# Longer pauses between the steps that make a recurrence chunk's operands

## The chip, the core and the metric

The kernel runs on one core of a Trainium2 chip. The metric is the device time of one execution in microseconds (us). The engines are TensorE (PE: matrix products and transposes), VectorE (DVE), ScalarE (ACT), GpSimd (POOL) and SyncE (SP, which here issues DMAs); each runs its own list of instructions in order, and they wait for each other through semaphores.

## The reference, cut to what matters

One layer of an encoder on 2112 tokens: 2048 of a new stream and 64 of a running one. A projection P = h @ w_in feeds a gated short convolution, an RWKV-7 recurrence and two gates; their merged output and a feed-forward network follow.

```python
h  = rms_norm(x);  proj = h @ w_in                    # 1024 -> 5376 columns
def step(s, inp):                                     # RWKV-7, per token, 8 heads of 64
    r_t, w_t, k_t, v_t, a_t, b_t = inp
    sa = einsum('bhij,bhj->bhi', s, a_t)
    s  = s * w_t + sa[..., None] * b_t + v_t[..., None] * k_t
    return s, einsum('bhij,bhj->bhi', s, r_t)
m = sigmoid(gate_A) * (conv(proj) @ w_conv_out) + sigmoid(gate_B) * (rwkv(proj) @ w_rwkv_out)
x = x + rms_norm(m @ w_o)
x = x + rms_norm((silu(up_1) * up_2) @ w_down)        # up = rms_norm(x) @ w_up
```

## The kernel before

The work has two stages. The first (`phase_a`, to about 1482 us) computes the projections and the whole recurrence. The second merges the branches and does the feed-forward part; the change does not touch it.

**The projections** are the fillers of the first stage. Their inputs are split into a high and a low half, so each product is three matmuls `mm` with 264 columns (`mm3`). A unit of one output column block and one half of a token quarter is 24 such matmuls, and the generator `projections` gives the turn back after every 12. Per column block, a weight tile is loaded by SP (`w_raw`), cast by ACT (`w_hi`) and subtracted by DVE (`w_lo`); evictions go to ACT and DVE. Between units DVE also adds pairs of feed-forward weights (`sw`, line 606, `weight_sums`).

**The recurrence** works on chunks of 64 tokens, two chunks to a group, 16 groups and a last one of a single chunk. Each group goes through three generators:
- `scan_prep` makes a chunk's operands. DVE scales the rows into `ar` and `bk` (line 700 to 705; bk's tile is named `v`). A pause follows. PE multiplies them, `pa<-ar,v` and `tr<-ar,v` (136), and DVE masks the result into `aa` and `aq` (716). A second pause follows. PE transposes `bk` (`tr<-cpack,v`), which needs the buffer `tr` that the masks have read, and computes `pu<-uv,aa`.
- `scan_solve` inverts 32x32 blocks by 31 pairs of small DVE operations (`tm`, `ti`, lines 760 and 762), sends them through DRAM (`asc`, `al`, `ttsc`, `tinv`), transposes a part (`d`, 776) and finishes with two products on PE (`pu<-d,aa`, `pu<-tinv`), each evicted by ACT (783, 790).
- `scan_chain` carries the state from chunk to chunk: `gy<-st,ar`, an add on DVE (`ysq`, 817), `pu<-ysq,tinv`, a copy on ACT (`uv`, 822), `pu<-uv,bkt`, `gy<-uv,aq`, a copy on ACT (`yt`, 837); then a norm on DVE and ACT and the transposes `tr<-cpack,yt`.

`phase_a` interleaves the three streams and the fillers by a counter, `self.t`. Every matmul adds its estimated length to it (`mm`, `transpose`), and a stream that yields a number gets its next turn when the counter has risen by that much since its turn began. So a pause is so much PE work, not time. A group's `scan_prep` may start when its projections are stored and the group two before it is through its chain. The order in which the code emits instructions gives their priority; a scheduler then settles each engine's list. When the fillers are used up, the counter rises by itself.

PSUM buffers `pa`, `tr`, `pu` and `gy` are single.

Of the kernel before, what the change touches and what calls it, by code (L numbers as in the profile page):

```python
# [34 lines left out]
WBUFS, KSTEP = 3, 4  # L35

YE, YT = 4, 10

PASSES = ((0, True, True, range(16)), (1, True, True, range(2)), (2, True, True, range(4)), (3, True, True, range(16)), (1, False, False, range(2, 16)), (2, False, False, range(4, 16)))
MIX = {1: 0, 3: 1, 10: 1}  # L40
# [45 lines left out]
class Trunk:  # L86
# [583 lines left out]
    def scan_prep(self, grp, nxt):  # L670


        nc, pool = self.nc, self.sp
        nch = grp["nch"]
        n = nch * CH
        if "sg" not in grp:
            self.scan_load(grp)
            yield 9
        if "ep" not in grp:
            self.scan_decays(grp)  # L680
        en, ep, v, r = grp["sg"], grp["ep"], grp["v"], grp["r"]
        ks = grp["ks"].rearrange("p (c s) t -> p c s t", s=3)
        kk, b_, kf = ks[:, :, 0], ks[:, :, 1], ks[:, :, 2]
        vt = self.tr()
        for p in range(4):
            self.transpose(vt[0:n, p, :], v[:, p, :], self.ident)
        uvs = []
        for c in range(nch):
            uv = pool.tile([P, 4, P], F32, name="uv", bufs=4)
            nc.scalar.copy(out=uv[64:128], in_=vt[c * CH:c * CH + CH])  # L690
            uvs.append(uv)
        yield 1
        epv = ep.rearrange("p (c j) t -> p c j t", j=nch)
        asc = self.dram.tile([nch * 16, CH // 2, CH // 2], F32, name="asc", bufs=2)
        chunks = grp["chunks"] = []
        for c in range(nch):
            t0 = c * CH
            uv = uvs[c]
            ar = pool.tile([P, 4, P], F32, name="ar", bufs=4)
            nc.vector.scalar_tensor_tensor(out=ar[:, :, 0:CH], in0=kk[:, :, t0:t0 + CH], scalar=-1.0, in1=epv[:, :, c, 0:CH],  # L700
                                           op0=ALU.mult, op1=ALU.mult)
            nc.vector.tensor_tensor(out=ar[:, :, CH:P], in0=r[:, :, t0:t0 + CH], in1=epv[:, :, c, 1:CH + 1], op=ALU.mult)
            bk = pool.tile([P, 4, P], F32, name="v", bufs=1)
            nc.vector.tensor_tensor(out=bk[:, :, 0:CH], in0=b_[:, :, t0:t0 + CH], in1=en[:, :, t0:t0 + CH], op=ALU.mult)
            nc.vector.tensor_tensor(out=bk[:, :, CH:P], in0=kf[:, :, t0:t0 + CH], in1=en[:, :, t0:t0 + CH], op=ALU.mult)
            yield 4
            aa = pool.tile([P, 8, CH], F32, name="aa", bufs=4)
            aq = pool.tile([P, 8, CH], F32, name="aq", bufs=4)
            pas = (self.psum.tile([P, 4, P], F32, name="pa", bufs=1), self.tr())
            for p in range(4):  # L710
                for b in range(2):
                    rows = slice(64 * b, 64 * b + 64)
                    self.mm(pas[b][:, p, :], bk[rows, p, :], ar[rows, p, :], start=True, stop=True)
            for b in range(2):
                for t, s0 in ((aa, 0), (aq, CH)):
                    nc.vector.tensor_tensor(out=t.rearrange("p (c b) t -> p c b t", b=2)[:, :, b, :], in0=pas[b][:, :, s0:s0 + CH],
                                            in1=self.amask[:, s0:s0 + CH].unsqueeze(1).broadcast_to([P, 4, CH]), op=ALU.mult)
            yield 4
            z = self.tr()
            for p in range(4):  # L720
                self.transpose(z[:, p, :], bk[:, p, :], self.ident)
            bkt = pool.tile([P, 4, P], F32, name="bkt", bufs=4)
            nc.scalar.copy(out=bkt, in_=z)
            cc = pool.tile([P, 4], F32, name="cc", bufs=4)
            nc.gpsimd.tensor_copy(out=cc, in_=epv[:, :, c, CH])
            for b in range(2):
                s0 = (b * nch + c) * 8
                nc.sync.dma_start(out=asc[s0:s0 + 8].rearrange("s u t -> u s t"),
                                  in_=aa[32 * b:32 * b + 32, :, 32 * b:32 * b + 32])
            pu = self.pu()  # L730
            for s in range(8):
                self.mm(pu[0:64, s, :], aa[64:128, s, :], uv[64:128, s // 2, (s % 2) * 64:(s % 2) * 64 + 64], start=True, stop=True)
            nc.scalar.copy(out=uv[0:64], in_=pu[0:64].rearrange("t (p h) i -> t p (h i)", h=2))
            chunks.append(dict(uv=uv, ar=ar, aa=aa, aq=aq, bkt=bkt, cc=cc))
            yield 1
        grp["asc"] = asc
        while nxt is not None and self.ready < nxt["off"] + nxt["nch"] * CH:
            yield 1
        if nxt is not None:
            self.scan_load(nxt)  # L740
            yield 9
            self.scan_decays(nxt)
# [743 lines left out]
```

## Time and profile before

| | us |
|---|---|
| median of 3 timed runs | 3283.89 |
| lowest, highest | 3279.99, 3292.36 |
| the profiled execution | 3272.44 |
| its span | 3270.7 |

The mean granted TensorE clock of the profiled execution is 0.981 of full speed. Times in the rows are counted from the start of its span. A matmul of the trace is shown with the time until its last result, so one that takes 0.28 us is followed by the next 0.12 us after its start.

### The profile page before, as it was taken

What the parts mean: (1) busy time and instruction counts of PE and PEld (TensorE: products, weight loads), DVE (VectorE), ACT (ScalarE), POOL (GpSimd) and SP (SyncE); (2) the same over time, 40 slices, a digit from 0 to 9 for tenths busy, and PEclk for the clock granted to TensorE, in tenths of its full rate; (3) what the DMA queues carried; (4) which work ended last, traced back from release to release, by engine and by line L of the source; (5) the groups of instructions that cost most, each with busy time, mean ns of one, the idle gap of its engine ahead of it and who ended that gap; (6) DMA issues with size and microseconds to landing.
All of it is one profiled execution on the core that took longest, in us unless ns stands there. A gap on an engine that the chain in (4) does not pass through costs nothing.

```text
span 3270.7 us, 64324 instructions
## 1 busy us (share of the span) xinstructions
PE 3119.1 (95%) x23060; PEld 3043.3 (93%) x23060; DVE 2375.4 (73%) x5091; ACT 1736.6 (53%) x3418; POOL 488.2 (15%) x906
## 2 busy tenths in 40 slices
PE   6999999999999999998999999999999999999997
PEld 6989899998889999998999989999999999999997
DVE  5866787887878778746576876776867776866657
ACT  7534664664575446534433455556645466544454
POOL 2400132132124101000000011210011200111100
PEclk9999999999999999999999999999999999999999
DMA  5787578766767677647475467778777887766675
GB/s 163 221 246 230 184 222 252 218 202 206 222 212 208 205 236 233 190 125 248 125 233 160 137 227 231 248 254 260 228 224 224 264 254 236 234 190 191 191 253 169
DMA packets 526226, 699.52 MB, mean 214 GB/s; under 512 B 111137, under 2 KB 358497, under 8 KB 525905
## 3 DMA queue, kind: packets, MB, share of 16 engines
q1 hardware_dynamic: 468528, 592.67, 59.5%
q0 software_dynamic: 25456, 72.20, 6.0%
q10 hardware_dynamic: 31920, 30.54, 2.8%
q8 instruction: 181, 2.97, 0.4%
q14 instruction: 141, 1.15, 0.1%
HBM read 522.10 MB, written 173.12 MB: 213 GB/s over the span
## 4 chain that ended last, share of the span: by engine, by line
issue 38%; PE 16%; POOL 5%; DMA 3%; DVE 2%; ACT 0%; POOLq 0%; SPq 0%; DVEq 0%; ACTq 0%
PE mm L136 14%; POOL tp_s L1229 3%; PE pu L136 1%; DMA x<-x_s 1%; POOL x_s L1088 1%; PE gy L136 1%; POOL out_y L1088 1%; POOL nb_s L1173 0%; DMA nb_s<-x 0%; DMA x_s<-r 0%; DMA gt_s<-psv 0%; DMA tp_s<-f 0%; DVE ti L762 0%; DMA out_y<-r 0%; DVE w_lo L150 0%
## 5 line engine op out<-in xcount | busy, mean ns | idle before, releaser
L136 PE MATMUL mm<-h_hi,w_hi 128*128 128x264 f32 (+1 forms) x5112 | 1586.3, 311 | 55.8 <-DVE f L1248 20.9
L136 PE MATMUL mm<-h_hi,w_lo 128*128 128x264 f32 (+1 forms) x5112 | 1558.1, 305 | 8.9 <-DVE w_lo L150 5.6
L136 PE MATMUL mm<-h_lo,w_hi 128*128 128x264 f32 (+1 forms) x5112 | 1559.5, 305 | 3.4 <-DVE h_lo L217 2.8
L136 PEld LDWEIGHTS mm<-h_hi,w_hi 128*128 128x128 f32 x5112 | 973.6, 191 | 81.6 <-DVE f L1248 25.0
L136 PEld LDWEIGHTS mm<-h_hi,w_lo 128*128 128x128 f32 x5112 | 974.7, 191 | 12.6 <-DVE w_lo L150 7.8
L136 PEld LDWEIGHTS mm<-h_lo,w_hi 128*128 128x128 f32 x5112 | 975.2, 191 | 7.7 <-DVE h_lo L217 3.6
L188 ACT CAST w_hi<-w_raw 128x512 fp32r<-128x512 f32 (+1 forms) x810 | 487.8, 608 | 535.4 <-PE mm L136 322.5
L189 DVE TENSOR_TENSOR w_lo<-w_raw,w_hi 128x512 fp32r<-128x512 f32 (+1 forms) x810 | 540.4, 674 | 259.9 <-ACT w_hi L188 251.7
L136 PE MATMUL mm<-t_hi,w_hi 128*128 128x352 f32 x1116 | 360.8, 323 | 1.7 <-ACT mm L1330 1.7
L136 PE MATMUL mm<-t_lo,w_hi 128*128 128x352 f32 x1116 | 358.0, 321 | 0.0
L136 PE MATMUL mm<-t_hi,w_lo 128*128 128x352 f32 x1116 | 358.0, 321 | 0.0
L150 DVE TENSOR_TENSOR w_lo<-w_raw,w_hi 128x1024 fp32r<-128x1024 f32 x168 | 207.5, 1236 | 116.6 <-ACT w_hi L149 112.6
L149 ACT CAST w_hi<-w_raw 128x1024 fp32r<-128x1024 f32 x168 | 175.7, 1047 | 135.1 <-PE mm L136 88.0
L136 PEld LDWEIGHTS mm<-t_hi,w_hi 128*128 128x128 f32 x1116 | 209.4, 188 | 2.6 <-ACT mm L1330 2.3
L1229 POOL DMA_DIRECT2D tp_s<-f x231 | 125.5, 543 | 576.8 <-DVE f L1248 337.1
L136 PEld LDWEIGHTS mm<-t_lo,w_hi 128*128 128x128 f32 x1116 | 209.7, 188 | 0.3
L136 PEld LDWEIGHTS mm<-t_hi,w_lo 128*128 128x128 f32 x1116 | 209.5, 188 | 0.0
L189 DVE TENSOR_TENSOR t_lo<-d,t_hi 128x352 fp32r<-128x352 f32 x198 | 97.6, 522 | 72.5 <-ACT t_hi L188 71.5
L188 ACT CAST t_hi<-d 128x352 fp32r<-128x352 f32 x198 | 91.5, 486 | 89.7 <-DMA d<-tp_s 83.9
L760 DVE TENSOR_TENSOR tm<-al,ti 128x60 f32<-128x60 f32 (+27 forms) x527 | 118.9, 226 | 10.7 <-DMA al<-asc 2.7
L762 DVE TENSOR_TENSOR ti<-ti,tm 128x60 f32<-128x60 f32 (+27 forms) x527 | 117.7, 223 | 8.5
L606 DVE TENSOR_TENSOR sw<-sw 128x512 f32<-128x512 f32 (+1 forms) x136 | 95.3, 701 | 20.4 <-DMA sw<-in_w_up 16.0
(207 smaller groups left out, 3731.7 us busy)
## 6 DMA issues: line engine op xcount, KB each, us to landing
w_raw<-in_w_in SPq DMA_DIRECT2D x168, 512.0 KB, 4.4
w_raw<-us_s SPq DMA_DIRECT2D x264, 256.0 KB, 3.2
w_raw<-in_w_up SPq DMA_DIRECT2D x198, 256.0 KB, 3.1
tp_s<-f POOLq DMA_DIRECT2D x231, 176.0 KB, 3.6
d<-tp_s SPq DMA_DIRECT2D x105, 352.0 KB, 3.9
w_raw<-ds_s SPq DMA_DIRECT2D x96, 256.0 KB, 3.5
sw<-in_w_up SPq DMA_DIRECT2D x88, 256.0 KB, 4.7
us_s<-sw SPq DMA_DIRECT2D x88, 256.0 KB, 3.6
```

Source lines behind the costliest of these rows:

```text
L136: self.nc.tensor.matmul(out, lhsT, rhs, **kw)
L149: nc.scalar.copy(out=hi[:, :kt], in_=raw[:, :kt])
L150: nc.vector.tensor_tensor(out=lo[:, :kt], in0=raw[:, :kt], in1=hi[:, :kt].bitcast(F32), op=ALU.subtract)
L188: nc.scalar.copy(out=hi, in_=x)
L189: (eng or nc.vector).tensor_tensor(out=lo, in0=x, in1=hi.bitcast(F32), op=ALU.subtract)
L606: nc.vector.tensor_tensor(out=w[x], in0=w[x], in1=w[y], op=ALU.add)
L760: nc.vector.tensor_tensor(out=tv, in0=al[0:np_, u, u + 1:32].unsqueeze(1).broadcast_to([np_, k, m]), in1=ti[0:np_, 0:k, u:u + 1].broadcast ...
L762: nc.vector.tensor_tensor(out=tu, in0=tu, in1=tv, op=ALU.add)
L1088: (nc.sync if rows else nc.gpsimd).dma_start(out=dst[d, :, t0:t0 + n], in_=x)
L1229: nc.gpsimd.dma_start(out=self.tp_s[TP[op], i], in_=x)
```

## The change

The two pauses of `scan_prep` inside a chunk, between the scaling and the products and between the masks and the transposes, go from 4 to a new constant `YP` = 7. Nothing else is edited.

```diff
 YE, YT = 4, 10
+
+YP = 7
...
             nc.vector.tensor_tensor(out=bk[:, :, CH:P], in0=kf[:, :, t0:t0 + CH], in1=en[:, :, t0:t0 + CH], op=ALU.mult)
-            yield 4
+            yield YP
...
                                             in1=self.amask[:, s0:s0 + CH].unsqueeze(1).broadcast_to([P, 4, CH]), op=ALU.mult)
-            yield 4
+            yield YP
             z = self.tr()
```

Lines behind the edit move down by 2. In the built program the distances change everywhere in the first stage. PE's list in the middle of it, at the end of the solve of the twelfth group; before, fillers stand around the second product:

```order
L136 MATMUL mm<-h_hi,w_lo 128x264
L136 MATMUL pu<-tinv 32x32 x16
L136 MATMUL mm<-h_hi,w_hi 128x264
L136 MATMUL mm<-h_lo,w_hi 128x264
L136 MATMUL mm<-h_hi,w_lo 128x264
```

And now:

```order
L138 MATMUL mm<-h_hi,w_lo 128x264
L138 MATMUL pu<-tinv 32x32 x16
L142 MATMUL tr<-cpack,v 128x128 x4
L138 MATMUL mm<-h_hi,w_hi 128x264
L138 MATMUL mm<-h_lo,w_hi 128x264
L138 MATMUL pu<-uv,aa 64x64 x8
```

The next group's second chunk has moved back until its last steps meet the solve's products of the group before.

PE's list at the end of the first stage, where the 128x352 matmuls are the first of the next stage. Before, the last group's output transposes stand behind fillers:

```order
L136 MATMUL mm<-h_hi,w_hi 128x264
L136 MATMUL mm<-h_lo,w_hi 128x264
L136 MATMUL mm<-h_hi,w_lo 128x264
L140 MATMUL tr<-cpack,yt 128x64 x4
L136 MATMUL mm<-h_hi,w_hi 128x352
```

And now:

```order
L138 MATMUL mm<-h_hi,w_lo 128x264
L138 MATMUL pu<-d_20513,aa 32x32 x8
L138 MATMUL pu<-tinv 32x32 x8
L142 MATMUL tr<-cpack,yt 128x128 x4
L138 MATMUL gy<-st_107,ar 128x128 x4
L138 MATMUL pu<-ysq,tinv 64x64 x8
L138 MATMUL pu<-uv,bkt 128x128 x4
L138 MATMUL gy<-uv,aq 64x64 x8
L142 MATMUL tr<-cpack,yt 128x64 x4
L138 MATMUL mm<-h_hi,w_hi 128x352
```

The last group's solve products and chain stand behind the last filler; before, they had fillers between them.

DVE's list at the same place, from the last operation of the last group's solve (64 partitions) on. Before:

```order
L762 TENSOR_TENSOR ti<-ti,tm 64x8
L830 TENSOR_TENSOR stmp<-pu,st_108 64x256 x2
L833 TENSOR_TENSOR st_107<-stmp,cc 64x4x64 x2
L843 TENSOR_REDUCE s_19893<-yt 128x8
L844 SCALAR_TENSOR_TENSOR yt<-s_19893,yt 128x512
L850 TENSOR_REDUCE s_19938<-ysq 128x8
L853 RECIPROCAL s_19938<-s_19938 128x8
L854 TENSOR_TENSOR yt<-yt,s_19938 128x512
L776 STREAM_TRANSPOSE d_20352<-tinv 32x256
```

And now:

```order
L764 TENSOR_TENSOR ti<-ti,tm 64x8
L819 TENSOR_TENSOR ysq<-gy,uv 64x512
L832 TENSOR_TENSOR stmp<-pu,st_107 64x256 x2
L835 TENSOR_TENSOR st_108<-stmp,cc 64x4x64 x2
L778 STREAM_TRANSPOSE d_20513<-tinv 32x256
L819 TENSOR_TENSOR ysq<-gy,uv 64x512
L832 TENSOR_TENSOR stmp<-pu,st_108 64x256 x2
L835 TENSOR_TENSOR st_107<-stmp,cc 64x4x64 x2
L845 TENSOR_REDUCE s_20396<-yt 128x8
```

Both chain steps of the group before the last have moved behind the last group's solve, the second of them also behind the transpose `d`.

## Rows read from the trace of the kernel before

**Rows 1.** The page, part 1: busy us, share of the span, instructions

```profile
PE 3119.1 (95%) x23060; PEld 3043.3 (93%) x23060; DVE 2375.4 (73%) x5091; ACT 1736.6 (53%) x3418; POOL 488.2 (15%) x906
```

**Rows 2.** PE's waits, 160 to 1485 us: us in total, times, longest

```profile
PE tr L140 <- DVE aq L716: 12.7, 6, 5.4
PE pa L136 <- DVE v L705: 9.1, 9, 3.4
...
PE tr L140 <- DVE tm L760: 3.9, 3, 2.0
...
PE pu L136 <- DVE aa L716: 3.4, 5, 1.2
PE tr L140 <- DVE ti L762: 3.1, 3, 1.2
```

**Rows 3.** Timeline of PE: start, us, instruction, [idle before <-releaser]

```profile
179.45 1.09 PE L140 MATMUL tr<-cpack,v 128*128 128x128 f32 x4 [5.44 <-DVE aq L716]
...
537.50 1.09 PE L140 MATMUL tr<-cpack,v 128*128 128x128 f32 x4 [4.36 <-DVE aq L716]
```

**Rows 4.** Timeline of DVE before the first of these waits

```profile
175.27 0.69 DVE L606 TENSOR_TENSOR sw<-sw 128x512 f32<-128x512 f32 x1 [6.22 <-DMA sw<-in_w_up]
```

**Rows 5.** Stretches: us, busy PE, PEld, DVE, ACT, POOL, PEclk, DMA share, GB/s

```profile
170.00:190.00 20.00, 14.56 (x118) 13.67 (x118) 11.28 (x22) 5.45 (x8) 2.84 (x2) 0.83 0.83 263
530.00:550.00 20.00, 15.64 (x119) 14.74 (x119) 16.77 (x36) 9.81 (x18) 1.83 (x6) 0.83 0.88 266
890.00:920.00 30.00, 26.50 (x179) 23.88 (x178) 19.00 (x54) 19.09 (x48) 3.96 (x14) 0.77 0.68 186
640.00:1130.00 490.00, 459.66 (x4146) 435.12 (x4146) 406.37 (x1053) 277.50 (x558) 124.61 (x241) 0.97 0.70 211
1440.00:1460.00 20.00, 20.00 (x166) 20.00 (x166) 4.90 (x4) 6.08 (x11) 0.18 (x1) 1.00 0.39 120
```

**Rows 6.** PE's waits, 640 to 1130 us

```profile
PE pa L136 <- DVE v L705: 7.9, 6, 3.4
PE mm L136 <- ACT w_hi L149: 4.8, 3, 2.9
...
PE pu L136 <- DVE aa L716: 2.5, 3, 1.2
...
PE tr L140 <- DVE ti L762: 2.4, 2, 1.2
...
PE tr L140 <- DVE aq L716: 0.6, 2, 0.5
PE tr L140 <- DVE tm L760: 0.5, 1, 0.5
```

**Rows 7.** Timeline of PE at the stage's end, without the fillers

```profile
1462.92 0.69 PE L136 MATMUL pu<-d,aa 32*32 32x32 f32 x16
...
1468.84 1.05 PE L136 MATMUL gy<-st,ar 128*128 128x128 f32 x8
1471.29 1.14 PE L136 MATMUL pu<-ysq,tinv 64*64 64x64 f32 x16
1473.93 1.05 PE L136 MATMUL pu<-uv,bkt 128*128 128x128 f32 x8
...
1481.97 0.43 PE L140 MATMUL tr<-cpack,yt 64*128 64x64 f32 x4 [1.33 <-DVE yt L854]
```

**Rows 8.** ACT: tile tinv (ns least/median/most), and the last chain's copy

```profile
L783 ACT COPY tinv<-pu x17: 362/575/579, 258.8 to 1463.8; 32x512 f32<-32x512 f32 x16, 32x256 f32<-32x256 f32 x1
...
1476.10 0.58 ACT L837 COPY yt<-gy 64x512 f32<-64x512 f32 x1 [3.04 <-PE gy L136]
```

**Rows 9.** Timeline of DVE: the last solve's first and last operation, the transpose

```profile
1398.67 0.17 DVE L760 TENSOR_TENSOR tm<-al,ti 64x31 f32<-64x31 f32 x1
...
1421.11 0.17 DVE L762 TENSOR_TENSOR ti<-ti,tm 64x8 f32<-64x8 f32 x1
...
1430.14 0.43 DVE L776 STREAM_TRANSPOSE d<-tinv 32x256 f32<-32x256 f32 x1 [1.47 <-DMA tinv<-ttsc]
```

## The prediction

> **What bounds the kernel now.** I began with the page [rows 1]: the reader sees TensorE (PE) at 95% of the span, VectorE (DVE) at 73%. The end is set by PE, so the change is worth what it adds to or takes from PE's idle time and slow clock. The edit touches only the first stage, up to about 1482 us, so I read PE's waits from 160 us (first chunk) to 1485 us. Five of its entries belong to the steps between which the pauses lie [rows 2]: the products `pa` waiting for `bk` (named v there), the transposes `tr` of `bk` waiting for the masks (named aq, tm or ti, whichever ran last on DVE), and `pu<-uv,aa` waiting for aa. Together 12.7 + 9.1 + 3.9 + 3.4 + 3.1 = 32.2 us. That is all the change can give back in waits.
>
> Next I asked why DVE was late, since a pause cures some causes and not others.
> - The two longest waits, 5.44 and 4.36 us [rows 3], are one cause. DVE sat for 6.22 us at a weight-sum addition whose DMA had not landed [rows 4], and the masks stood behind it.
> - From 640 to 1130 us DVE is busy 406 of 490 us [rows 5], and 7.9 + 2.5 + 2.4 + 0.6 + 0.5 = 13.9 us of the waits fall there [rows 6]: a backlog.
> - The rest, 32.2 - 9.8 - 13.9 = 8.5 us, is plain shortness of the pause.
>
> Third come the clock and the end of the stage. After long waits the granted clock drops: 0.83 over 170 to 190 us and 530 to 550 us, 0.77 over 890 to 920 us [rows 5], a mix of TensorE's two levels, 1.2 and 2.4 GHz. At the stage's end PE has projection matmuls ("fillers") to run beside the last group's recurrence almost to its last instruction; it waits there only 1.33 us [rows 7].
>
> **The change part by part.** No instruction is added or removed; only places move. The pauses count from before the step's own PE work. In the built order the products now stand mostly 72 to 84 fillers behind the group's first transposes or the previous chunk's, where 30 to 48 was common, and the transposes of bk stand 48 fillers behind the products instead of 24. A filler costs 20.00 / 166 = 0.12 us [rows 5], so the second pause gains 24 x 0.12 = 2.9 us, the first at least as much.
>
> 1. Waits behind the late DMA: 2.9 us off each of two, -5.8 us. Between 0 (the additions fall elsewhere, and as badly) and -9.8.
> 2. Waits in the backlog: a consumer that comes later finds DVE done, but DVE's work stays, and the next thing PE needs of it (low weight halves, evictions) waits instead. I take half, -7.0 us; bounds 0 and -13.9.
> 3. The short waits, the longest 2.0 us [rows 2], lie inside the added slack: -8.5 us; bounds -8.5 and 0.
> 4. Clock: the three stretches lose 20 x 0.17 + 20 x 0.17 + 30 x 0.23 = 13.7 us of full-speed work. The waits ahead of them shrink, but other waits stand beside them. I take half, -6.9 us; bounds 0 and -13.7.
> 5. A new neighbourhood. The single PSUM buffer `pu` now passes from the solve's second product to `pu<-uv,aa` with two fillers and four transposes between, in four groups; elsewhere 6 or more fillers lie between. The eviction in between takes 0.58 us on ScalarE (ACT) [rows 8] against some 2 x 0.12 + 0.43 us of cover (the nearest transposes [rows 7]), and its queue can hold it longer. I charge +2.5 us; bounds 0 and 5.
> 6. The end of the stage. Each group takes some 25 to 45 fillers more, and there are only so many. In the new order all projection matmuls are gone before the last group's solve products: these, that group's whole chain step and the previous group's output transposes stand one behind the other on PE with nothing between. I count from the last filler, F, with durations of the same steps. The previous chain's gy ends 24 fillers, 2.9 us, before F; from its copy at 1476.10 to the end of the output transposes at 1481.97 + 0.43 it took 6.3 us [rows 7, 8], so the transposes end at F + 3.6 (0.2 us for the copy to start). Then gy 1.05, DVE's add with its two hand-overs 0.9, pu 1.14, ACT's copy 0.7, the two last products 1476.10 - 1473.93 = 2.2 [rows 7, 8]: F + 9.6. Then 6.3 again: F + 15.9. The PE work inside is 2 x 0.69 + 2 x 0.43 + 1.05 + 1.14 + 2.2 = 6.6 us, so PE idles 9.3 us, where it idled 1.33: +8.0 us. DVE has a new order there too: the add that the previous chain needs stands behind all of the last group's solve, and the next add behind the transpose `d`, which waits for a trip through DRAM. In the trace 1430.14 + 0.43 - 1421.28 = 9.3 us pass from the solve's last operation to the end of that transpose [rows 9]; PE has 36 fillers (4.3 us) and 1.14 + 2.2 + 1.05 us of chain steps to run meanwhile, 8.7 us. About even, so I charge 1.5 us, and 1.3 us for small products at the lower clock: +10.8 us. Bounds 6 (the DVE order costs nothing and copies overlap better) and 20.
>
> The Trainium skill bears on step 6. Row: after the waits named above, 0.83 and 0.77 were granted [rows 5]. "TensorE: Matmul & The Clock Gate", section "What's actually happening", says that the throttled clock is the default and activity releases it. By that rule the bare end of the stage runs at 1.2 GHz throughout, doubling its 6.6 us of small products; the sum would be some 5 us worse. The trace agrees for long waits, but no row shows small products that trickle like this.
>
> Everything after this stage is the same program and starts behind the last chain as before; I cost it at nothing. If its first loads come sooner relative to the chain's end, that is a gain of at most a few us, left in the range.
>
> **Sum**: -5.8 - 7.0 - 8.5 - 6.9 + 2.5 + 10.8 = -14.9 us. The profiled execution ran 3272.44 us, so it would take 3257.5; it stands 11.5 us under the median of the timed runs, 3283.89. The same step from the median: 3269.0 us, 0.45% less.
>
> **Rivals.**
> - *All waits vanish.* For it: the slack added is 2.9 us and more, and most waits are under that. Against: the two longest exceed it, and DVE is 83% busy where 13.9 us of them lie. -32.2 - 13.7 + 8.0 = -37.9 us: about 3246.
> - *The waits only move.* DVE's backlog sets the pace in the passages where PE waits, and the late DMA meets another instruction. Only the short waits go: -8.5 + 2.5 + 10.8 = +4.8 us: about 3289. For it: PE also waits 4.8 us on w_hi in the same stretch [rows 6], the same crowding under another name. Against: DVE has 84 us free there.
> - *The end of the stage costs more* (slower). One mechanism: the last group's solve ends late on DVE, and the previous chain's add stands behind it. Its price is one to one from the point where the solve's last operation falls behind PE's arrival at `pu<-ysq` of that chain; PE's cover from the products' block is 216 fillers, 26 us. A solve in its backlog could start 10 to 15 us later; then the end costs 20 to 25 us and, with only the short waits gone, 3283.9 - 8.5 + 2.5 + 23 = 3301 us. The solve took 22.4 us from 1398.67 to 1421.11 beside other work [rows 9], which is near the cover.
> - *The pauses do nothing*, the scheduler putting things back: excluded for the places shown, which moved by 24 fillers; 3284 us.
>
> The Trainium skill has a rule here as well. Row: DVE leaves 84 of 490 us free, yet PE waits on it [rows 5, 6]. "Perfetto Trace Analysis", section "Optimization Strategy", says to find what blocks the engine and make that dependency start sooner or finish faster. This change does neither: it only lets the consumer come later, and by that rule the gain lasts while fillers last, which is what step 6 charges; wholly followed, it gives the second rival's time.
>
> **How the numbers follow.** Forecast (3259 to 3279) 0.36, all vanish 0.28, waits move 0.20, the end costs more 0.12, nothing 0.04. A measurement of this kernel tells 0.5%, 16.4 us, from no change: faster is under 3267.5, slower over 3300.3. Faster: 0.28 and 0.40 of the forecast's 0.36, 0.42. Slower: the late end and a little of the moved waits, 0.14. The same: 0.44. The forecast's own range is 3259 to 3279; for 8 in 10 I go from just past the first rival, 3244, to the third, 3301.
>
> **What would show it.** Right: the five entries of PE's waits fall from 32 to about 11 us, the granted clock of 500 to 950 us rises, and at the end of the stage PE idles about 10 us among the last group's chain steps, its fillers having ended some 16 us before. Step 2 is wrong if PE's waits on w_lo, w_hi or psv grow by as much as those fall; step 5 if `pu<-uv,aa` waits for tinv's copy by more than 5 us; step 6 if the last fillers to last transposes take over 22 us or under 12. The whole is wrong if PE's idle time between 160 and 1400 us does not shrink.

## The result: slower, outside the range

The changed kernel takes 3307.91 us (median of 6 runs, 3299.79 to 3311.82), the kernel before, beside it, 3280.89: a ratio of 1.0087 with a 95% interval of 1.0072 to 1.0103. That is 27 us slower; forecast was 3269, with a range of 3244 to 3301. The profiled executions stand further apart, 3311.82 against 3272.44 us, so what follows is read for where the time went; sizes come from the ratios. Line numbers of the changed kernel are the old ones plus 2.

**The waits moved, all of them.** TensorE's busy time on the page, beside [rows 1], and its waits from 160 to 1485 us, beside [rows 2]:

```profile
PE 3139.8 (95%) x23060; PEld 3065.3 (93%) x23060; DVE 2385.0 (72%) x5091; ACT 1745.8 (53%) x3427; POOL 492.3 (15%) x906
```

```profile
PE pu L138 <- DVE d L778: 14.9, 5, 4.3
...
PE tr L142 <- DVE yt L856: 5.4, 3, 3.0
...
PE pu L138 <- ACT tinv L785: 4.3, 5, 1.7
PE tr L142 <- DVE aq L718: 3.9, 3, 2.4
...
PE pu L138 <- ACT tinv L792: 3.1, 4, 2.0
PE pa L138 <- DVE v L707: 2.9, 1, 2.9
...
PE tr L142 <- DVE tm L762: 1.4, 2, 1.1
```

The five entries of the preparation fell from 32.2 to 3.9 + 2.9 + 1.4 = 8.2 us. But the solve's products now wait on the transpose `d` (14.9, before 0), other products in the buffer `pu` on the copies into tinv (7.4, before 0), and the output transposes on yt (5.4, before 2.1). Added up over every row of this view the waits are 61.1 us, as before. (One trace is not exact to a microsecond: `ownyr` below, with the changed kernel's pauses, has 54.4, and four runs below with the old pauses have 58.3 to 61.7.)

Why does the product on `d` wait? VectorE and the DMA queue SP (start, us, instruction, [idle before <-releaser]) at one of the two long waits:

```profile
1303.95 0.17 DVE L764 TENSOR_TENSOR ti<-ti,tm 128x8 f32<-128x8 f32 x1
...
1310.11 0.32 SPq L772 DMA_DIRECT2D tinv<-ttsc  x1
...
1310.58 1.23 DVE L152 TENSOR_TENSOR w_lo<-w_raw,w_hi 128x1024 fp32r<-128x1024 f32 x1 [4.47 <-ACT w_hi L151]
...
1312.71 0.42 DVE L718 TENSOR_TENSOR aq<-tr,cpack 128x256 f32<-128x256 f32 x1
1313.05 0.69 DVE L778 STREAM_TRANSPOSE d<-tinv 32x512 f32<-32x512 f32 x1
```

```profile
1313.88 1.88 PE L138 MATMUL pu<-d,aa 32*32 32x32 f32 x32 [4.10 <-DVE d L778]
```

The next group's masks and a late weight half stand straight ahead of `d`, but they hardly hold it: its data, on their way through DRAM since the solve's last operation at 1303.95, land at 1312.84, and `d` starts 0.21 us later. At the other long wait a weight half holds it for 1.7 us (its data land at 791.50), and at a shorter one VectorE stands idle for the data:

```profile
792.09 1.23 DVE L152 TENSOR_TENSOR w_lo<-w_raw,w_hi 128x1024 fp32r<-128x1024 f32 x1 [2.34 <-ACT w_hi L151]
793.23 0.69 DVE L778 STREAM_TRANSPOSE d<-tinv 32x512 f32<-32x512 f32 x1
...
1101.91 0.70 DVE L778 STREAM_TRANSPOSE d<-tinv 32x512 f32<-32x512 f32 x1 [1.59 <-DMA tinv<-ttsc]
```

```profile
793.98 1.91 PE L138 MATMUL pu<-d,aa 32*32 32x32 f32 x32 [4.34 <-DVE d L778]
```

In the five late cases `d` starts 0.02 to 1.7 us after its data have landed. Nor is the solve slower: its 31 pairs take 39.5 us in the median group, before 42.8, and the trip through DRAM 6.9 to 10.5 us, before 6.6 to 12.7. What changed is TensorE's side. In the five late cases PE comes to the product 5.7 to 8.0 us behind the solve's last operation; before it never came sooner than 9.5. They are the groups 4, 7, 10, 11 and 14. Between such a group's preparation (its last `pu<-uv,aa`) and its `pu<-d,aa` PE's list now has 474, 430, 410, 374 and 395 fillers of 0.12 us; before it had 453, 461, 449, 462 and 424. So in four of the five the product was moved ahead of its data. In group 4 it was not; there the solve starts some 8 us later behind its preparation. Why the longer pauses leave fewer fillers in the solve's stretch is not shown.

**The clock.** Stretches after (busy us of PE, PEld, DVE, ACT, POOL, PEclk, DMA share, GB/s); 890 to 920 and 640 to 1130 stand beside [rows 5]:

```profile
890.00:920.00 30.00, 23.69 (x198) 22.16 (x196) 27.98 (x80) 23.23 (x52) 6.22 (x16) 1.00 0.69 215
...
790.00:810.00 20.00, 16.02 (x131) 14.96 (x132) 4.49 (x8) 4.25 (x7) 0.00 (x0) 0.60 0.39 89
1310.00:1330.00 20.00, 16.12 (x145) 15.22 (x146) 5.62 (x10) 5.09 (x10) 0.00 (x0) 0.66 0.66 192
640.00:1130.00 490.00, 458.42 (x4128) 436.64 (x4125) 403.15 (x1009) 273.16 (x548) 121.35 (x239) 0.96 0.69 210
...
1490.00:1530.00 40.00, 16.51 (x110) 14.18 (x109) 15.17 (x28) 16.72 (x37) 7.01 (x8) 0.59 0.44 139
```

The old bad stretch of 890 to 920 runs at full clock. New ones stand behind the waits on `d` at 793.98 and 1313.88. Summed over stretches of 10 us from 160 to 1480, each times what its granted clock lacks to 1, the loss is 49.5 us; in the trace before it was 30.8. Part of this difference is chance: four runs below with the old pauses (`baretail`, `latetail`, `lateyr`, `lateown`) lose 39.1 to 40.9, and `ownyr`, with the new ones, 47.7. The mean granted clock of whole executions shows the drop without this doubt: 0.968 to 0.973 in the six runs of the changed kernel, 0.976 to 0.983 in 97 runs of the kernel before beside the experiments, without one that ran slow as a whole (3773 us).

**The end of the stage.** PE after, beside [rows 7]; the first row is the last filler:

```profile
1490.67 0.29 PE L138 MATMUL mm<-h_hi,w_lo 128*128 128x264 f32 x1
1490.89 0.69 PE L138 MATMUL pu<-d,aa 32*32 32x32 f32 x16
1492.03 0.69 PE L138 MATMUL pu<-tinv 32*32 32x32 f32 x16 [0.45 <-ACT tinv L785]
1494.65 1.11 PE L142 MATMUL tr<-cpack,yt 128*128 128x128 f32 x4 [1.93 <-DVE yt L856]
1495.55 1.91 PE L138 MATMUL gy<-st,ar 128*128 128x128 f32 x8
1504.17 1.97 PE L138 MATMUL pu<-ysq,tinv 64*64 64x64 f32 x16 [6.70 <-DVE ysq L819]
1506.81 2.08 PE L138 MATMUL pu<-uv,bkt 128*128 128x128 f32 x8 [0.67 <-ACT uv L824]
1508.81 1.97 PE L138 MATMUL gy<-uv,aq 128*64 128x64 f32 x16
1515.77 0.66 PE L142 MATMUL tr<-cpack,yt 64*128 64x64 f32 x4 [4.99 <-DVE yt L856]
```

From the last filler to the last transposes' end 25.8 us pass, where 15.9 were forecast. Two things are larger than in the forecast. The products take 1.91 to 2.08 us where they took 1.05 and 1.14 (granted clock 0.50, 1.2 GHz, from 1494 to 1510 us); the forecast had 1.3 us for this. And 6.70 us go to `pu<-ysq`, whose reason is on VectorE, beside [rows 9]:

```profile
1473.10 0.17 DVE L764 TENSOR_TENSOR ti<-ti,tm 64x8 f32<-64x8 f32 x1
...
1480.22 0.43 DVE L778 STREAM_TRANSPOSE d<-tinv 32x256 f32<-32x256 f32 x1 [0.39 <-DMA tinv<-ttsc]
...
1503.43 0.68 DVE L819 TENSOR_TENSOR ysq<-gy,uv 64x512 f32<-64x512 f32 x1 [8.84 <-DMA yr_s<-ysq]
```

The chain's sum, the norm's square and the output tile yr share one SBUF buffer, `ysq`. With the previous group's output transposes now right ahead of the last chain, its sum must wait until that output has been evicted, added to, multiplied and stored to DRAM. The last operation of the solve itself starts at 1473.10, in good time.

The two profiled executions divide alike. The last filler starts 10.3 us later than before, although some small products that stood among the fillers now stand behind it. From there to the first product of the next stage 29.2 us pass, before 5.7. The remaining 5.5 us of their distance stand behind that product, in the stage that the prediction costed at nothing; over all runs here that stage takes 1779 to 1790 us, and no run tells what moves it.

### The profile page after: what moved, and what is told of

Read it like the earlier page. It is cut to its first block, busy times and chain, and to the rows that moved or that the text cites. A ratio compares the mean times of both kernels' runs of the same rounds, so it can differ in the third digit from the quotient of the medians.

```text
span 3310.0 us, 64343 instructions
## 1 busy us (share of the span) xinstructions
PE 3139.8 (95%) x23060; PEld 3065.3 (93%) x23060; DVE 2385.0 (72%) x5091; ACT 1745.8 (53%) x3427; POOL 492.3 (15%) x906
## 3 DMA queue, kind: packets, MB, share of 16 engines
q14 instruction: 141, 1.16, 0.1%
## 4 chain that ended last, share of the span: by engine, by line
issue 41%; PE 10%; POOL 5%; DMA 2%; DVE 1%; ACT 1%; POOLq 0%; DVEq 0%; ACTq 0%; SPq 0%
PE mm L138 8%; POOL tp_s L1231 3%; PE pu L138 1%; POOL x_s L1090 1%; DMA tp_s<-f 1%; POOL out_y L1090 1%; POOL nb_s L1175 0%; PE gy L138 0%; DMA x<-x_s 0%; DMA d<-tp_s 0%; DVE w_lo L191 0%; PE tr L142 0%; DMA w_raw<-in_w_up 0%; ACT w_hi L190 0%; DVE f L1198 0%
```

## The experiments

Theory: the pauses do what was forecast to the preparation's waits, but lengthen each group's lap (from its preparation through its chain to the next that may start), so that the recurrence comes late; the price is a crowded end of the stage and, in the body (the first stage ahead of that end), waits on `d` with slow clock behind them. Rivals: the end alone; the body alone; one of the two pauses alone. Ratios are to the kernel before, beside it on the same chip; A, B and C are the rival outcomes of each expectation.

**Long pauses in the first six groups** (`six`, the edit in both places).

```diff
-            yield YP
+            yield YP if grp["off"] < 768 else 4
```

> The longer pauses only in the first six groups; the last three keep 4, so that all fillers last as long as before and the end of the stage is not bare. A (body and end both cost): the body's loss stays for two thirds of the groups: TensorE still waits on d and tinv at the solve's end (about 8 us on d) and the granted clock still sags in the windows near 430, 510, 790 and 1030 us; the end costs what it did before. 3288 to 3296 us, against 3281 before and 3308 with the change. B (the bare end alone costs): 3270 to 3279 us, since the waits of the preparation are gone and nothing has come in their place. C (the body alone costs): 3300 to 3308 us.

There are 17 groups, not nine as this text supposes: eleven keep 4, so it tests the early third only. Ratio 1.0001 (0.9980 to 1.0021). The early groups cost nothing that is seen (-7 to 7 us): six of them put off the last solve by 24 fillers only, and from the eleventh group on the solve has its 420 fillers and more, as before.

**The output tile in its own buffer** (`ownyr`).

```diff
-        yr = pool.tile([P, 4, n], F32, name="ysq", bufs=1)
+        yr = pool.tile([P, 4, n], F32, name="yr", bufs=1)
```

> The changed kernel, with the output tile yr in an SBUF buffer of its own instead of the one that it shares with the chain's sum and the norm's square. A (at the bare end the chain's sum waits for the store of the group before): VectorE's wait of 8.84 us on the store goes, TensorE's 6.70 us ahead of pu<-ysq falls to about 1 us, the last transposes come 5 to 7 us sooner: about 3301 us. B (the store only hides another wait that ends as late, as the transposes of the group before or the solve): within 2 us of the changed kernel, 3306 to 3310 us.

1.0069 (1.0046 to 1.0093). In its trace PE idles 0.93 us ahead of the last `pu<-ysq`, and the time from the last filler to the last transposes' start falls from 25.1 to 17.8 us. That is A's direction and size, 6 us, though the two intervals overlap.

**The end bare, the body as before** (`baretail`).

```diff
-        yield 6
+        yield 6 if nch == 2 else 6 + LATE      # LATE = 40
```

> The kernel before, with 40 more of pause ahead of the last group's solve, so that this solve's products and the last chain stand behind all fillers; the body is as before. The output of the group before is stored long ahead, so its store cannot hold the last sum. A (a bare end costs what step 6 of the prediction charged, and the rest of the changed kernel's loss is the store and the body): 3289 to 3294 us, and from the last filler to the last transposes about 15 us. B (a bare end is dear by itself, as its small products run at 1.2 GHz and every hand-over counts): 3297 to 3305 us, over 22 us. C (the end costs nothing, all is the body): 3279 to 3284 us.

1.0007 (0.9987 to 1.0027). PE at the end, last filler and last transposes:

```profile
1479.75 0.29 PE L138 MATMUL mm<-h_hi,w_lo 128*128 128x264 f32 x1
...
1494.55 0.66 PE L142 MATMUL tr<-cpack,yt 64*128 64x64 f32 x4 [5.55 <-DVE yt L856]
```

It is 15.5 us by the trace, close to the 15.9 of step 6, yet the run costs 2 us (-4 to 9), as C has it. So a bare end of this kind is not the loss.

**Preparation may start sooner** (`through`).

```diff
+        grp["through"] = True          # in scan_chain, behind the chunks
-            ... and done["chain"] >= m - 1
+            ... and (m < 2 or "through" in groups[m - 2])
```

> The changed kernel, but a group's preparation may start when the chunks of the group two before are through, not only its norm and its output as well: this takes back the filler work that the longer pauses add to each group's lap. A (the loss is the longer lap: a later solve end and a bare end): the end of the stage holds only the last solve's products and the last chain, as in the run with a bare end; waits of the preparation stay low; 3285 to 3296 us. B (the loss is that the longer preparation crowds VectorE ahead of the transpose d, whatever the lap): TensorE still waits over 12 us on d and tinv in the body and the clock sags: 3300 to 3308 us. C (all of the loss was the end): 3270 to 3282 us.

0.9996 (0.9979 to 1.0012): with both pauses at 7 in all groups the loss is gone. From the eleventh to the sixteenth group a lap (from one `pu<-d,aa` to the next) is 372 to 388 fillers; before it was 350 to 397, with the change 400 to 428. B's time falls, although the product on `d` still waits 10.3 us here; A was too dear. The time is C's, although this end is bare too.

**The changed kernel's end behind the body of before** (`latetail`, and with yr's own buffer, `lateown`).

```diff
-        yield 6
+        yield 6 + LATE if grp["off"] == SEQ - P else 6      # LATE = 50
```

> The kernel before, with the solve of the last full group (of 17 groups the sixteenth) put off by 50 more of pause, so that the end of the stage has the changed kernel's order, from this group's solve products to the last transposes, behind the body of before with its pauses of 4. The buffer of yr is the shared one. A (the whole loss is the crowded end: late chain, store of the group before, small products at 1.2 GHz): from the last filler to the last transposes about 25 us, ratio to before 1.005 to 1.009 (16 to 29 us). B (the end costs little, as with the bare end that was run, ratio 1.0007, and the late groups of the body with their wait of 4 us on d and the slow clock after it cost the rest): ratio 1.000 to 1.003.

> The kernel before with the sixteenth group's solve put off (ratio 1.0049 as it was run), now with a buffer of its own for yr: the body of before and the crowded end of the changed kernel, without the store in its way. A (the store is 6 to 7 us of the end's cost): no wait ahead of the last pu<-ysq over 1.5 us, last filler to last transposes about 17 us, ratio 1.002 to 1.004. B (the store's place is taken by another wait): ratio 1.0045 to 1.006.

1.0049 (1.0030 to 1.0068), and 1.0038 (1.0026 to 1.0050) with the buffer. PE at the last chain, first of `latetail`, then of `lateown`:

```profile
1496.62 1.97 PE L138 MATMUL pu<-ysq,tinv 64*64 64x64 f32 x16 [6.68 <-DVE ysq L819]
...
1508.21 0.66 PE L142 MATMUL tr<-cpack,yt 64*128 64x64 f32 x4 [4.98 <-DVE yt L856]
```

```profile
1490.98 1.94 PE L138 MATMUL pu<-ysq,tinv 64*64 64x64 f32 x16 [0.98 <-DVE ysq L819]
...
1502.47 0.66 PE L142 MATMUL tr<-cpack,yt 64*128 64x64 f32 x4 [4.91 <-DVE yt L856]
```

The wait on the store is made by the order of the end alone and goes with the buffer (A of `lateown`); what it is worth in time is not resolved, since the two intervals overlap. The crowded end costs 0.0049 x 3276 = 16 us (10 to 22), the larger part of the 27, but not the whole: neither A nor B of `latetail` holds alone. The same kernel once more (`lateyr`, a single execution, 3298.23 us) has a wait of 7.5 us ahead of the last `pu<-ysq` and 24.5 us to the last transposes' start.

> A second look at the kernel before with the sixteenth group's solve put off, whose ratio was 1.0049: whether the wait of 6.7 us ahead of the last pu<-ysq and the half speed of the small products at the end come back as they were. If the store is what holds VectorE there, it does: 6 to 7 us, and 24 to 26 us from the last filler to the last transposes.

**Long pauses in six late groups** (`late6`, the edit in both places).

```diff
-            yield YP
+            yield YP if 1152 <= grp["off"] < 1920 else 4
```

> The longer pauses only in the tenth to the fifteenth of the 17 groups, where they lengthen each group's lap; the end is bare for the last solve's products and the last chain only, and no store is in its way. A (the crowded end is the loss): like the run with a bare end, ratio 0.999 to 1.003. B (the late groups of the body cost: a wait on d of some 4 us and a sagging clock between 1130 and 1480 us): ratio 1.004 to 1.007, and the granted clock between 1130 and 1480 us at 0.97 instead of 1.00.

1.0039 (1.0022 to 1.0055), where the same kind of bare end cost 1.0007: some 10 us (2 to 19) lie in the body. There, on VectorE and on PE:

```profile
1083.17 0.42 DVE L718 TENSOR_TENSOR aq<-pa,cpack 128x256 f32<-128x256 f32 x1
1083.50 0.69 DVE L778 STREAM_TRANSPOSE d<-tinv 32x512 f32<-32x512 f32 x1
```

```profile
1084.33 1.88 PE L138 MATMUL pu<-d,aa 32*32 32x32 f32 x32 [6.81 <-DVE d L778]
```

Here the data land at 1080.59, and other work of VectorE, two masks of 0.3 us each at its end, holds `d` for 2.9 us of the 6.8; PE came 3.1 us before the data. From the preparation to the product on `d` the six groups have 374 to 432 fillers, before 420 to 462. The granted clock from 1130 to 1480 us loses 10.3 us, as in the changed kernel; the kernel before and the four runs with its pauses lose 0 to 3.4. B holds, at the near edge of its range.

**One pause at a time** (`second`, `first`): `YP` in one of its two places, 4 in the other.

> Only the second of the two pauses at 7 (between the products pa and the transposes of bk), the first at 4. The lap grows by about half as much, the previous group's output leaves 200 fillers before the last, so only the last solve's products and the last chain stand bare. A (the crowded end is the loss): ratio 0.999 to 1.003, with the waits tr on aq, tm and ti gone and those of pa on v still there. B (each pause costs by its length, half of the change's loss each): ratio 1.004 to 1.005.

> Only the first of the two pauses at 7 (ahead of the products pa), the second at 4; the counterpart of the run with only the second, which came out at 0.997. A (the lap has slack for about half of the added pause, the other half comes late; it does not matter which pause it is): 0.995 to 1.000, with pa's waits on v gone and the transposes' waits on aq, tm and ti still there. B (the first pause is the harmful one, since it moves the masks onto the end of the solve on VectorE): 1.003 to 1.008, with waits on d of over 8 us in all.

0.9970 (0.9952 to 0.9987) and 1.0001 (0.9988 to 1.0014). Neither half is harmful; the second pause alone is a gain of 10 us, better than either rival of that run allowed. Together they lose 27. So the costs don't add. The reading is that half the pause fits into the slack of the lap: the output of the sixteenth group still leaves 168 fillers or more before the last, where with both it falls behind all of them. In `first` the waits on `d` are 1.7 us, so its rival B falls.

**Faster solve steps** (`fastsolve`): the changed kernel with `YE` 3 instead of 4.

> The changed kernel with one number changed: the solve's steps are 3 apart instead of 4, which shortens a group's solve by 7 units of pause and lets the last group's come sooner; both pauses at 7, yr in the shared buffer, preparation starts as before. The last output transposes of the group before stand 48 fillers ahead of the bare end, which holds the last solve and chain only. A (the recurrence comes late, and the end is the larger part of the loss): ratio 0.998 to 1.003; the waits on d in the body stay. B (solve steps closer together make VectorE later, as more of its work falls in the same time): 1.004 to 1.010.

1.0017 (1.0001 to 1.0033), A. The shorter lap, and with it an end without the previous group's output, takes back most of the loss, although the waits on `d` grow to 19.1 us and the clock up to 1480 us still loses 46.0. So waits on `d` alone don't make the loss.

**The lap restored, and room ahead of `d`** (`balance`); the same with both pauses at 4 (`bal4`); the same with 10 ahead of `d` (`bal10`).

```diff
-YE, YT = 4, 10
+YE, YT = 3, 14          # and the edits of ownyr and through
```

> The changed kernel with the lap taken back to that of before: preparation may start when the chunks of the group two before are through, the solve's steps are 3 apart instead of 4, the pause ahead of the transpose d is 14 instead of 10, and yr has its own buffer. The last solve and chain then stand where they stood before, under fillers to the end, and d comes later after its trip through DRAM. A (the pauses are good, the lap was the loss): PE's waits of the preparation and on d both under 12 us in all, end as before: 3262 to 3272 us, ratio 0.995 to 0.999. B (VectorE's work, not its place, sets the waits; solve steps closer together crowd it): other waits grow by as much, ratio 0.999 to 1.003. C (the longer preparation hurts by itself): over 1.004.

> The fastest kernel so far (ratio 0.9951: own buffer for yr, preparation let start by the chunks, solve steps 3 apart, 14 ahead of d) with both pauses back at 4: what the pauses alone are worth where the lap does not suffer. A (the pauses are good where the lap allows them): the preparation's waits come back, about 25 us of them; ratio 0.999 to 1.004. B (the gain came from the solve and the start of the preparation, the pauses are worth nothing): 0.994 to 0.997.

> The fastest kernel (ratio 0.9951) with the pause ahead of the transpose d back at 10 instead of 14; its end is under fillers as well. A (with preparation longer, VectorE comes to d late and the consumer must come later too; d's waits cost time and clock in the body): waits on d of 12 us or more, ratio 0.998 to 1.002. B (only the lap and the end count): ratio 0.993 to 0.997, whatever d waits.

`balance` 0.9951 (0.9934 to 0.9969), 3260.78 us: faster than both kernels. `bal4` 1.0017 (1.0003 to 1.0030), `bal10` 1.0023 (1.0006 to 1.0040). From 160 to 1130 us, for `balance`, `bal4` and `bal10`:

```profile
160.00:1130.00 970.00, 933.51 (x8434) 892.39 (x8433) 778.74 (x1959) 544.92 (x1064) 201.23 (x391) 0.99 0.72 222
```

```profile
160.00:1130.00 970.00, 917.37 (x8261) 874.46 (x8261) 772.18 (x1949) 537.74 (x1049) 192.88 (x388) 0.98 0.71 217
```

```profile
160.00:1130.00 970.00, 924.90 (x8146) 882.59 (x8145) 761.72 (x1931) 537.56 (x1053) 204.66 (x386) 0.96 0.71 217
```

The pauses alone (`bal4` against `balance`) are worth 0.0066, 22 us, where the rest leaves them room: PE is busy 16 us more in this stretch, and its five waits (160 to 1485 us) fall from 34.8 to 9.6 us. Taking away the room ahead of `d` loses it again (0.0072, 24 us). Up to 1440 us, as `balance` ends its first stage at 1457, PE waits 36.5 us in `balance` and 51.4 in `bal10`, and the clock loses 13.7 and 46.1 us. On `d`, `balance` first:

```profile
PE pu L138 <- DVE d L778: 5.0, 4, 1.8
```

```profile
PE pu L138 <- DVE d L778: 11.6, 6, 2.8
```

The edit of `bal10` shortens the lap as well (180 fillers are left behind its last transposes, none in `balance`), so the room ahead of `d` is not alone in it. Two stretches of `bal10` behind such waits (2.82 us at 689.74, 2.81 us at 1190.08):

```profile
690.00:700.00 10.00, 10.00 (x107) 9.25 (x104) 4.27 (x9) 4.64 (x10) 0.18 (x1) 0.66 0.25 74
...
1190.00:1200.00 10.00, 9.92 (x97) 9.23 (x98) 2.33 (x3) 2.40 (x5) 0.00 (x0) 0.50 0.84 242
```

PE is busy and still slow: the wait is paid twice. Of the 46.2 us that `bal10` loses to the clock up to 1480 us, 25.7 stand in stretches at or straight behind five of its six waits on `d` (the sixth, 1.24 us at 974.88, has none). The traces together say that the solve's end costs clock more readily than other waits of that length. Of PE's waits of 1 to 3 us from 160 to 1440 us in all sixteen traces, with no other above 0.9 us within 12 us of them, 19 are on `d`, and from 1 us ahead of them to 12 us behind their end 3.9 us of clock are lost on the average (over 1 us in 18 of 19); for the 167 others it is 1.1 us (over 1 us in 81). No run isolates why.

## Why the prediction was wrong

- **Steps 1 to 3** were right for the waits that they name: -21.3 us forecast, -24.0 measured. The two waits behind the late DMA shrank from 9.8 us to one of 2.4, the longest of that entry; the backlog's, from 640 to 1130 us, from 13.9 to 5.1; the short ones from 8.5 to the rest, 0.7. `balance` against `bal4` shows this gain as time.
- **The step that failed is the one that let this gain stand in the sum.** "The next thing PE needs of it waits instead" was charged in step 2 alone, to half of the backlog and to weight halves and evictions. It holds for the whole: the 24 us came back, as 25.6 us more on `d`, tinv and yt. The second rival said that waits only move, with the wrong instructions: the waits on w_lo, w_hi and psv, which step 2 named as the place, fell. The prediction's own sign for the whole, PE's idle time up to 1400 us, did not shrink.
- **Step 4** has the wrong sign: the clock was to give back 6.9 us and took 18.7 more than in the trace before, 8.6 to 10.4 more than in the four other traces with the old pauses. The granted clock of 500 to 950 us, which was to rise, is 0.95 in both.
- **Step 5** was right in size: PE's wait ahead of the next group's `pu<-uv,aa` for the solve's last eviction is 3.1 us, forecast 2.5. It left out the product on `d`, which opens the same end of a solve.
- **Step 6** worked out a bare end of 15.9 us; alone that end measures 15.5 and costs 2 us. But the order that the step describes, with the previous group's output transposes in it too, is another: 25.8 us, over the 22 that the prediction named as its sign of being wrong. The missing term is the single buffer `ysq`, 6.7 us of wait by the trace and 4 to 6 us by the ratios (0.0049 - 0.0038, 0.0087 - 0.0069, each of them with intervals that overlap); products at 1.2 GHz add some 3.5 us (four that take 1.91 to 2.08 us for 1.05 to 1.15), where 1.3 was charged. By `latetail` the end is 16 us, forecast 10.8.
- **The third rival**, 3301 us, came nearest in time, by a mechanism that did not occur: the last solve was not late on VectorE. That its time is near is luck.

So the 27 us are 16 of the end (shown by putting that end behind the old body) and 11 (4 to 20) of the body, by subtraction; `late6` shows some 10 us in the body by itself. `through`, which takes the lap back and with it the loss, points to the longer lap behind both. How much of the body's part is waits on `d` and how much their clock, group by group, stays open.

The prediction cited the Trainium skill, "Perfetto Trace Analysis", section "Optimization Strategy", on making a dependency start sooner or finish faster. The trace of the change agrees with that rule: letting only the consumer come later left the sum of waits at 61.1 us. The other runs agree in part: the largest gain came where `balance` also let the preparation and the solve start sooner, but `bal4`, which does so with the old pauses, gained nothing (1.0017), and `second`, which only lets one consumer come later, gained 10 us.

It also cited "TensorE: Matmul & The Clock Gate" of the Trainium skill, section "What's actually happening", for a bare end throttled throughout. The chain's products in the changed kernel's end agree, with 1.91 to 2.08 us each; `late6`, whose bare end ran the same products in 1.14 to 1.16 us, does not.

## What to carry to other kernels

A pause that lets a consumer come later is free only as long as the loop that contains it has slack: here each of two pauses alone cost nothing, and both cost 27 us. Before lengthening one, count what work then stands between the other producers and their consumers (here the product on `d` came ahead of its data), and give that step room too. A late instruction should be compared with the time at which its own data arrived before its neighbours in the list are blamed. And where a step is moved next to another, list every buffer that the two share, with the store that must land before it is free.

## What was not expected of the hardware

- Five of the six waits of 1 to 3 us on the solve's transpose in `bal10` have stretches beside or straight behind them in which PE is busy 8 to 10 of 10 us at a granted clock of 0.50 to 0.84: 11.6 us of waits with 25.7 us of clock loss.
- The same row of small products, with no wait over 0.7 us in it, ran at 2.4 GHz in `late6` (granted clock 1.00 from 1495 to 1500 us) and in part at 1.2 GHz in `baretail` (0.50 from 1484 to 1489); the runs don't tell why. One product of it, first in `late6`, then in `baretail`:

```profile
1497.56 1.16 PE L138 MATMUL pu<-uv,bkt 128*128 128x128 f32 x8 [0.67 <-ACT uv L824]
```

```profile
1485.02 2.08 PE L138 MATMUL pu<-uv,bkt 128*128 128x128 f32 x8 [0.67 <-ACT uv L824]
```
